# Two weight combinations of the MLP's up projection made by accumulating DMAs, with the signs of the seven-product scheme turned

## The chip, the cores and the metric

The kernel runs on one core of one Trainium2 chip. Its time is the device time of one execution in microseconds; before the change three runs took 1085.81, 1086.14 and 1086.2 us, with a median of 1086.14 us. The profile is of one more execution of the same program. Matrix products run on PE (TensorE), elementwise work on DVE (VectorE) and ACT (ScalarE); POOL (GpSimd) and SP (SyncE) issue DMAs or do small things. Each engine works through its own queue in the order in which the program put its instructions, and engines wait for each other and for DMAs by semaphores.

## The reference

The program is a decoder trunk of two layers over 512 tokens and a width of 1024: one layer with multi-head latent attention, one with gated linear attention, each followed by a squared-ReLU MLP with 4096 hidden units. Only the MLP is touched:

```python
def sq_relu_mlp(xn, w_up, w_down):
    hid = jnp.square(jax.nn.relu(xn @ w_up))
    return hid @ w_down

for i in range(DEPTH):                      # DEPTH = 2
    ...                                     # x = x + mixer(rms_norm(x))
    x = x + sq_relu_mlp(rms_norm(x, norm_mlp[i]), mlp_w_up[i], mlp_w_down[i])
return rms_norm(x, final_norm)
```

`w_up` is 1024x4096 and `w_down` 4096x1024 in each layer, all float32.

## The kernel before

**Precision.** Every float32 operand of a product is split into a rounded high part (`wh`, written by ACT with a Copy, L104) and the rest (`wl`, written by DVE with a subtraction, L107). An ordinary product then takes three matmuls (`mm3`, L109: high by high, high by low, low by high).

**The MLP.** `mlp` (L793) cuts the 4096 hidden units into eight blocks of 512. The first block's up projection is done plainly by `up` (L801). Meanwhile `quadrants` (L890) combines the four quadrants of the normed activations (two halves of the width by two halves of the tokens) into four combinations, in four `comb` tiles `t1` to `t4`, and splits each into a kept tile `T1` to `T4` (L904 to L907). The seven other blocks go through `up_fast` (L909). It does the block's up projection by the two-by-two scheme of Winograd, with seven products instead of eight. The block's weights are four quadrants of 512x256: `a11` and `a12`, the upper and lower half of the first loaded tile `raw[0]`, and `a21` and `a22`, the halves of `raw[1]`. DVE makes four combinations of them:

- `s1 = a21 + a22` (L958) and `s2 = s1 - a11` (L959), each in a `comb` tile;
- `s4 = a12 - s2` (L969) in a third `comb` tile;
- `a11 - a21` (L970), written over `a21`.

`product` (L916) splits one of the seven weight tiles and runs sixteen matmuls, eight with 512 columns (L923) and eight with 256 (L924). The order on PE is `a11`, one tile of the down projection, `a12`, `s2`, two down tiles, `a11 - a21`, `s1`, one down tile, `s4`, `a22`, four down tiles. These down tiles belong to the block before (`down`, L823; `others(n)` steps it n tiles on); each sums into a PSUM bank `b`, of which there are three, and DVE adds it to the residual `xT` (L837), which frees the bank. `total` (L934) and `finish` (L945) join the products, apply the ReLU and the row scale (L947), square, and split.

**Buffers and queues.** Weights come by SP's queue (`load`, L132), 1 MB each, into `wraw` with two buffers, and `raw` for one down chunk of each block. A load waits until DVE has made the last `wl` out of the tile that lay in its buffer. `wh` and `wl` have three buffers each, `comb` has four. In `up`, the two chunks of the plain block take two weight pieces each; the second piece of the second chunk has its `wl` made in the middle of PE's work on that chunk, and the load of the first fast block's `raw[1]` (SP, L134) waits for this `wl`, since it goes into the same buffer.

**Who sets the order.** A scheduler gives each engine its order when the program is built, by its own estimate of when operands are ready; program order only breaks ties. So an instruction can stand on an engine ahead of work that comes earlier in the text.

Of the kernel before, what the change touches and what calls it, by code (L numbers as in the profile page):

```python
# [14 lines left out]
AF = mybir.ActivationFunctionType  # L15
ALU = mybir.AluOpType
AX = mybir.AxisListType

P = 128
# [5 lines left out]
FB = 512  # L25
TH = S // 2
# [24 lines left out]
def trunk_kernel(ctx: ExitStack, tc: tile.TileContext, t_in: dict, out: bass.AP, out_row: bass.AP):  # L51
    nc = tc.nc
    PE, ACT, DVE, POOL, SP = nc.tensor, nc.scalar, nc.vector, nc.gpsimd, nc.sync
# [5 lines left out]
    def uname(s):  # L59
        count[0] += 1  # L60
        return f"{s}_{count[0]}"
# [17 lines left out]
    def two_banks(tag):  # L79
        return psum["pool"].tile([P, 1024], F32, tag=f"ps_{tag}", bufs=1, name=uname("ps2"))  # L80
# [8 lines left out]
    def tmp(shape=(P, 512), dt=F32):  # L89
        return sb.tile(list(shape), dt, tag="tmp", bufs=6, name=uname("tmp"))  # L90

    def slot(tag, shape=(P, 512)):
        return sb.tile(list(shape), F32R, tag=f"set_{tag}", bufs=16, name=uname("set"))
# [5 lines left out]
    def f(ap):  # L99
        return ap.bitcast(F32)  # L100

    def split(src, hi, lo, hi_eng=ACT, lo_eng=DVE, order=lambda i: i):
        if hi_eng is ACT:
            order(ACT.activation(hi, src, AF.Copy))  # L104
        else:
            hi_eng.tensor_copy(hi, src)
        lo_eng.tensor_tensor(lo, src, f(hi), ALU.subtract)  # L107
# [24 lines left out]
    def load(src, a, n):  # L132
        raw = sb.tile([P, a, n], F32, tag="wraw", bufs=2, name=uname("wraw"))
        SP.dma_start(raw, src)  # L134
        return raw

    def piece(raw, a, n, order=lambda i: i):
        hi = sb.tile([P, a, n], F32R, tag="wh", bufs=3, name=uname("wh"))
        lo = sb.tile([P, a, n], F32R, tag="wl", bufs=3, name=uname("wl"))
        split(raw, hi, lo, order=order)  # L140
        return hi, lo

    def cut(pair, *idx):
        return tuple(t[idx] for t in pair)
# [56 lines left out]
    def gcol(name, j):  # L201
        c = GAIN_COL[name] + j
        return gains[:, c : c + 1]
# [84 lines left out]
    nrm = Norm(ND, inv_dr, "mix", 0)  # L288
# [81 lines left out]
    def col_chunk(w2d, c0, n):  # L370
        return load(w2d[:, c0 : c0 + n].rearrange("(k p) n -> p k n", p=P), w2d.shape[0] // P, n)
# [421 lines left out]
    def mlp(layer, nrm, tag, nxt, final=False):  # L793
        w_up, w_dn = t_in["mlp_w_up"][layer], t_in["mlp_w_down"][layer]
# [88 lines left out]
        KH = ND // 2  # L883

        def comb():
            return fast.tile([P, KH, 256], F32, tag="comb", bufs=4, name=uname("comb"))
# [3 lines left out]
        def quadrants():  # L890
            lead, trail = range(KH), range(KH, ND)
            quad["11"] = [nrm.parts[k][:, :, first] for k in lead]
            quad["21"] = [nrm.parts[k][:, :, first] for k in trail]
            quad["22"] = [nrm.parts[k][:, :, second] for k in trail]
            t1, t2, t3, t4 = comb(), comb(), comb(), comb()
            for k in lead:
                g1, g2 = (gcol(nrm.g, nrm.g0 + j) for j in (k, k + KH))
                u, v = xT[k], xT[k + KH]
                ACT.activation(t3[:, k], u[:, second], AF.Copy, scale=g1)
                DVE.scalar_tensor_tensor(t3[:, k], v[:, second], g2, t3[:, k], ALU.mult, ALU.subtract)  # L900
                DVE.scalar_tensor_tensor(t2[:, k], u[:, first], g1, t3[:, k], ALU.mult, ALU.add)
                DVE.scalar_tensor_tensor(t4[:, k], v[:, first], g2, t2[:, k], ALU.mult, ALU.subtract)
                DVE.scalar_tensor_tensor(t1[:, k], v[:, second], g2, t2[:, k], ALU.mult, ALU.subtract)
            for name, t in (("T2", t2), ("T3", t3), ("T1", t1), ("T4", t4)):  # L904
                parts = fast.tile([P, KH, 2, TH], F32R, tag=name, name=uname(name))
                split(t, parts[:, :, 0], parts[:, :, 1])
                quad[name] = [parts[:, k] for k in lead]  # L907

        def up_fast(b, others):  # L909
            raw = [col_chunk(w_up, b * FB + c * 256, 256) for c in range(2)]  # L910
            a11, a12 = raw[0][:, :KH], raw[0][:, KH:]
            a21, a22 = raw[1][:, :KH], raw[1][:, KH:]
            halves = [(slot(tag), slot(tag)) for _ in range(4)]


            def product(t, a, q, start):  # L916
                w = piece(a, KH, 256)
                for j in range(2):
                    o = t[:, j * 512 : (j + 1) * 512]
                    for k in range(KH):  # L920
                        wh, wl = cut(w, slice(None), k, slice(j * P, (j + 1) * P))
                        x = quad[q][k]
                        PE.matmul(o.rearrange("p (h t) -> p h t", h=2), wh, x, start=start and k == 0, stop=False, skip_group_check=True)  # L923
                        PE.matmul(o[:, :TH], wl, x[:, 0], start=False, stop=k == KH - 1, skip_group_check=True)  # L924

            def parts(t):
                v = t.rearrange("p (j h t) -> p h j t", j=2, h=2)
                return v[:, 0], v[:, 1]

            def by_tile(v):  # L930
                return v.rearrange("p (j t) -> p j t", j=2)


            def total(t, term=None):  # L934
                high, low = parts(t)
                r = tmp()
                if term is None:
                    ACT.activation(by_tile(r), low, AF.Copy)
                else:
                    DVE.tensor_tensor(by_tile(r), low, by_tile(term), ALU.add)  # L940
                DVE.tensor_tensor(by_tile(r), high, by_tile(r), ALU.add)  # L941
                return r


            def finish(c, half, tk):  # L945
                c3 = by_tile(c)
                DVE.scalar_tensor_tensor(c3, c3, 0.0, nrm.rstd[:, tk].unsqueeze(1).to_broadcast([P, 2, TH]), ALU.max, ALU.mult)  # L947
                ACT.activation(c, c, AF.Square)
                for j in range(2):
                    hi, lo = halves[2 * half + j]  # L950
                    split(c3[:, j], hi[:, tk], lo[:, tk])

            z, y = two_banks("z"), two_banks("y")
            product(z, a11, "11", True)
            others(1)
            p1 = total(z)
            s1, s2 = comb(), comb()
            DVE.tensor_tensor(s1, a21, a22, ALU.add)  # L958
            DVE.tensor_tensor(s2, s1, a11, ALU.subtract)  # L959
            product(y, a12, "21", True)  # L960
            c11 = total(y, p1)
            product(z, s2, "T2", False)
            others(2)
            u = total(z)
            finish(c11, 0, first)
            s4 = comb()

            with tc.issue_after(quad["hid"]) if b == 1 else nullcontext():
                DVE.tensor_tensor(s4, a12, s2, ALU.subtract)  # L969
                DVE.tensor_tensor(a21, a11, a21, ALU.subtract)  # L970
            product(z, a21, "T3", False)
            v = total(z)
            y = two_banks("y")
            product(y, s1, "T1", True)
            others(1)
            c22 = total(y, v)
            product(y, s4, "22", False)
            product(z, a22, "T4", False)
            finish(c22, 1, second)
            c12 = total(y, u)  # L980
            finish(c12, 0, second)
            c21 = total(z)
            finish(c21, 1, first)
            others(4)
            return halves

        hid = up()
        quadrants()
        for b in range(NB):
            if b + 1 < NB:  # L990
                tiles = down(b, hid)

                def others(n):
                    for _ in range(n):
                        next(tiles)

                hid = up_fast(b + 1, others)
                continue
            es.close()
            if final:  # L1000
                psum_layout(False)
                down_final(b, hid)
            else:
                for _ in down(b, hid):
                    pass
# [571 lines left out]
```

## Time and profile before

| what | before |
|---|---|
| median of three runs | 1086.14 us |
| profiled execution, first to last instruction (span) | 1084.4 us |
| PE busy | 1075.7 us, 99% of the span |
| DVE busy | 859.6 us, 79% |
| ACT busy | 549.2 us, 51% |
| POOL busy | 43.4 us, 4% |
| moved by DMA | 101.61 MB, 94 GB/s on the mean |

What lies around the profiled span, 1086.1 less 1084.4, is 1.7 us. A row of a group gives the busy time and the mean length of one instruction, then the engine's idle time just before them and what ended most of it. A row of the timeline gives start, length, engine, line, operation and tiles, with the idle time before it in brackets. SPq is SP's queue: its rows are the issues of DMAs. PE overlaps one matmul with the next, so that the length of one (0.39 us for 512 columns) is more than the step from one start to the next (some 0.23 us).

### The profile page before, as it was taken

What the parts mean: (1) busy time and instruction counts of PE and PEld (TensorE: products, weight loads), DVE (VectorE), ACT (ScalarE), POOL (GpSimd) and SP (SyncE); (2) the same over time, 40 slices, a digit from 0 to 9 for tenths busy, and PEclk for the clock granted to TensorE, in tenths of its full rate; (3) what the DMA queues carried; (4) which work ended last, traced back from release to release, by engine and by line L of the source; (5) the groups of instructions that cost most, each with busy time, mean ns of one, the idle gap of its engine ahead of it and who ended that gap; (6) DMA issues with size and microseconds to landing.
All of it is one profiled execution on the core that took longest, in us unless ns stands there. A gap on an engine that the chain in (4) does not pass through costs nothing.

```text
span 1084.4 us, 14045 instructions
## 1 busy us (share of the span) xinstructions
PE 1075.7 (99%) x5372; PEld 909.5 (84%) x5372; DVE 859.6 (79%) x1426; ACT 549.2 (51%) x927; POOL 43.4 (4%) x72
## 2 busy tenths in 40 slices
PE   9999999999999999999999999999999999999997
PEld 7888888888888888888788888888888888888886
DVE  7899968987887887977686584569888797797875
ACT  7767654553453453455345736556445345344354
POOL 8310002000000000000000000000000000000000
PEclk9999999999999999999999999999999999999999
DMA  7311232142332332322322222232233233223122
GB/s 225 88 50 39 79 117 78 61 134 78 117 117 78 117 117 78 110 84 79 90 76 78 78 78 75 70 127 67 90 115 119 79 101 123 87 80 125 69 97 78
DMA packets 86195, 101.61 MB, mean 94 GB/s; under 512 B 7440, under 2 KB 64016, under 8 KB 86128
## 3 DMA queue, kind: packets, MB, share of 16 engines
q1 hardware_dynamic: 84320, 99.67, 28.5%
q10 hardware_dynamic: 1808, 1.05, 0.3%
q8 instruction: 42, 0.69, 0.3%
q14 instruction: 25, 0.20, 0.1%
HBM read 98.35 MB, written 2.10 MB: 93 GB/s over the span
## 4 chain that ended last, share of the span: by engine, by line
PE 97%; DVE 1%; DMA 0%; ACT 0%; issue 0%; SPq 0%; DVEq 0%; ACTq 0%
PE ps L112 21%; PE ps L114 21%; PE ps L113 21%; PE ps L923 17%; PE ps L924 9%; PE ps L1201 2%; PE ps L129 1%; PE ps L408 1%; PE ps L871 1%; PE ps L1272 0%; PE ps L671 0%; PE ps L1251 0%; PE ps L667 0%; PE ps L670 0%; DMA gains<-in_gains_dram 0%; PE ps L669 0%
## 5 line engine op out<-in xcount | busy, mean ns | idle before, releaser
L112 PE MATMUL ps<-set,wh 128*128 128x512 f32 x760 | 296.8, 391 | 0.0
L113 PE MATMUL ps<-set,wh 128*128 128x512 f32 x760 | 296.6, 390 | 0.0
L114 PE MATMUL ps<-set,wl 128*128 128x512 f32 x760 | 296.3, 390 | 0.0
L104 ACT ACTIVATE wh<-wraw 128x1024 fp32r<-128x1024 f32 x139 | 147.0, 1061 | 240.8 <-PE ps L113 115.2
L107 DVE TENSOR_TENSOR wl<-wraw,wh 128x1024 fp32r<-128x1024 f32 x139 | 169.9, 1222 | 41.8 <-ACT wh L104 41.5
L114 PEld LDWEIGHTS ps<-set,wl 128*128 128x128 f32 x760 | 142.7, 188 | 30.3 <-DVE wl L107 0.2
L112 PEld LDWEIGHTS ps<-set,wh 128*128 128x128 f32 x760 | 142.7, 188 | 29.8
L113 PEld LDWEIGHTS ps<-set,wh 128*128 128x128 f32 x760 | 142.8, 188 | 27.6
L923 PE MATMUL ps<-T,wh 128*128 128x512 f32 x448 | 157.5, 391 | 0.0
L924 PE MATMUL ps<-T,wl 128*128 128x256 f32 x448 | 126.2, 282 | 0.0
L923 PE MATMUL ps<-set,wh 128*128 128x512 f32 x336 | 119.9, 397 | 0.0
L923 PEld LDWEIGHTS ps<-T,wh 128*128 128x128 f32 x448 | 84.1, 188 | 18.2
L924 PE MATMUL ps<-set,wl 128*128 128x256 f32 x336 | 94.2, 280 | 0.0
L107 DVE TENSOR_TENSOR wl<-comb,wh 128x1024 fp32r<-128x1024 f32 x42 | 51.4, 1223 | 47.7 <-ACT wh L104 47.7
L837 DVE TENSOR_TENSOR xT<-ps,xT 128x512 f32<-128x512 f32 x120 | 82.3, 686 | 7.1 <-PE ps L114 7.1
L104 ACT ACTIVATE wh<-comb 128x1024 fp32r<-128x1024 f32 x42 | 44.6, 1061 | 83.2 <-PE ps L923 81.8
L924 PEld LDWEIGHTS ps<-T,wl 128*128 128x128 f32 x448 | 84.6, 189 | 0.5
L923 PEld LDWEIGHTS ps<-set,wh 128*128 128x128 f32 x336 | 63.1, 188 | 15.1
L941 DVE TENSOR_TENSOR tmp<-ps,tmp 128x512 f32<-128x512 f32 x98 | 67.2, 686 | 0.9
L924 PEld LDWEIGHTS ps<-set,wl 128*128 128x128 f32 x336 | 63.4, 189 | 1.6
L112 PE MATMUL ps<-wh,set 128*128 128x512 f32 x144 | 58.8, 408 | 0.0
L104 ACT ACTIVATE wh<-raw 128x1024 fp32r<-128x1024 f32 x28 | 29.6, 1055 | 56.7 <-PE ps L923 55.7
(362 smaller groups left out, 1662.3 us busy)
## 6 DMA issues: line engine op xcount, KB each, us to landing
wraw<-in_mlp_w_up_dram SPq DMA_DIRECT2D x32, 1024.0 KB, 5.4
wraw<-in_mlp_w_down_dram SPq DMA_DIRECT2D x18, 1024.0 KB, 5.0
raw<-in_mlp_w_down_dram SPq DMA_DIRECT2D x14, 1024.0 KB, 5.1
wraw<-in_gla_w_in_dram SPq DMA_DIRECT2D x12, 1024.0 KB, 5.2
wraw<-in_mla_w_o_dram SPq DMA_DIRECT2D x4, 1024.0 KB, 5.2
wraw<-in_gla_w_o_dram SPq DMA_DIRECT2D x4, 1024.0 KB, 5.2
xT<-in_x_dram SPq DMA_DIRECT2D x6, 256.0 KB, 5.1
wraw<-in_mla_w_in_dram SPq DMA_DIRECT2D x3, 512.0 KB, 7.1
```

The source lines that it names most:

```text
L104: order(ACT.activation(hi, src, AF.Copy))
L107: lo_eng.tensor_tensor(lo, src, f(hi), ALU.subtract)
L112: PE.matmul(psum, wh, xh, start=start, stop=False)
L113: PE.matmul(psum, wh, xl, start=False, stop=False)
L114: PE.matmul(psum, wl, xh, start=False, stop=stop)
L129: PE.transpose(psum, src, ident[: src.shape[0], : src.shape[0]])
L408: PE.matmul(p, w[:, i, j * P : (j + 1) * P], x, start=start, stop=stop)
L837: DVE.tensor_tensor(xT[m], p, xT[m], ALU.add)
L923: PE.matmul(o.rearrange("p (h t) -> p h t", h=2), wh, x, start=start and k == 0, stop=False, skip_group_check=True)
L924: PE.matmul(o[:, :TH], wl, x[:, 0], start=False, stop=k == KH - 1, skip_group_check=True)
L941: DVE.tensor_tensor(by_tile(r), high, by_tile(r), ALU.add)
L1201: PE.matmul(p[:, t - t0], k[:, t * P : (t + 1) * P], moving[:, t], start=True, stop=True)
```

## The change

`s1` is no longer made by DVE. A plain 512 KB load on SP's queue brings `a22` into a `comb` tile, and a DMA on POOL's queue with an accumulating write adds `a21` to it. In the same way `raw[1]` is loaded as before, and a second accumulating DMA from POOL adds `a11` onto its upper half, so that `s3 = a11 + a21` stands there. For these to be sums, signs are turned: `s1` is as it was, `s3` is a sum instead of a difference, `s2 = s1 + a11` and `s4 = a12 + s2`. The activations' combinations T2, T1 and T4 are negated when they are split, and the ReLU of the second half of a block takes the minimum instead of the maximum, since its sums come out negated before they are squared.

The changed lines move the numbers of what lies behind them: what was L947 is L958 after, L837 stays, L959 becomes L969, L969 becomes L979, L923 and L924 become L933 and L934, L940 and L941 become L950 and L951.

```diff
-            for name, t in (("T2", t2), ("T3", t3), ("T1", t1), ("T4", t4)):
+            for name, t, sign in (("T2", t2, -1.0), ("T3", t3, 1.0), ("T1", t1, -1.0), ("T4", t4, -1.0)):
                 parts = fast.tile([P, KH, 2, TH], F32R, tag=name, name=uname(name))
-                split(t, parts[:, :, 0], parts[:, :, 1])
+                hi, lo = parts[:, :, 0], parts[:, :, 1]
+                ACT.activation(hi, t, AF.Copy, scale=sign)
+                DVE.scalar_tensor_tensor(lo, t, sign, f(hi), ALU.mult, ALU.subtract)
                 quad[name] = [parts[:, k] for k in lead]
 
         def up_fast(b, others):
+            def quadrant(c, h):
+                cs = slice(b * FB + c * 256, b * FB + c * 256 + 256)
+                return w_up[h * KH * P : (h + 1) * KH * P, cs].rearrange("(k p) n -> p k n", p=P)
+
             raw = [col_chunk(w_up, b * FB + c * 256, 256) for c in range(2)]
+            s1 = comb()
+            SP.dma_start(s1, quadrant(1, 1))
             a11, a12 = raw[0][:, :KH], raw[0][:, KH:]
-            a21, a22 = raw[1][:, :KH], raw[1][:, KH:]
+            s3, a22 = raw[1][:, :KH], raw[1][:, KH:]
+            POOL.dma_start(s1, quadrant(1, 0), accum_op=ALU.add)
+            POOL.dma_start(s3, quadrant(0, 0), accum_op=ALU.add)
...
-                DVE.scalar_tensor_tensor(c3, c3, 0.0, nrm.rstd[:, tk].unsqueeze(1).to_broadcast([P, 2, TH]), ALU.max, ALU.mult)
+                clip = ALU.min if half else ALU.max
+                DVE.scalar_tensor_tensor(c3, c3, 0.0, nrm.rstd[:, tk].unsqueeze(1).to_broadcast([P, 2, TH]), clip, ALU.mult)
...
-            s1, s2 = comb(), comb()
-            DVE.tensor_tensor(s1, a21, a22, ALU.add)
-            DVE.tensor_tensor(s2, s1, a11, ALU.subtract)
+            s2 = comb()
+            DVE.tensor_tensor(s2, s1, a11, ALU.add)
...
             with tc.issue_after(quad["hid"]) if b == 1 else nullcontext():
-                DVE.tensor_tensor(s4, a12, s2, ALU.subtract)
-                DVE.tensor_tensor(a21, a11, a21, ALU.subtract)
-            product(z, a21, "T3", False)
+                DVE.tensor_tensor(s4, a12, s2, ALU.add)
+            product(z, s3, "T3", False)
```

## The prediction

> **What bounds the kernel now.** I read the page first: busy shares, the chain that ended last, and the groups of the changed stage.
>
> ```profile
> span 1084.4 us, 14045 instructions
> PE 1075.7 (99%) x5372; PEld 909.5 (84%) x5372; DVE 859.6 (79%) x1426; ACT 549.2 (51%) x927; POOL 43.4 (4%) x72
> ...
> PE 97%; DVE 1%; DMA 0%; ACT 0%; issue 0%; SPq 0%; DVEq 0%; ACTq 0%
> ...
> L923 PE MATMUL ps<-T,wh 128*128 128x512 f32 x448 | 157.5, 391 | 0.0
> L924 PE MATMUL ps<-T,wl 128*128 128x256 f32 x448 | 126.2, 282 | 0.0
> L923 PE MATMUL ps<-set,wh 128*128 128x512 f32 x336 | 119.9, 397 | 0.0
> ```
>
> PE carries 97% of the chain, and the products that the change feeds were issued with no idle time before them (the last column). Then I cut four fast blocks out of the first layer (one starts every 41.4 us); the columns are length of the stretch, then busy time and count for PE, weight loads, DVE, ACT and POOL, then clock, DMA share and GB/s.
>
> ```profile
> 205.00:246.30 41.30, 41.30 (x209) 35.09 (x208) 36.44 (x50) 20.68 (x32) 0.00 (x0) 1.00 0.30 102
> 246.30:287.70 41.40, 41.40 (x209) 35.19 (x208) 32.90 (x45) 18.49 (x28) 0.00 (x0) 1.00 0.32 102
> 287.70:329.10 41.40, 41.40 (x209) 35.18 (x208) 35.21 (x47) 18.48 (x27) 0.00 (x0) 1.00 0.31 102
> 329.10:370.50 41.40, 41.40 (x209) 35.19 (x208) 33.92 (x46) 18.50 (x27) 0.00 (x0) 1.00 0.32 102
> ```
>
> PE is busy through every block at full clock. DVE's load differs by 3.5 us between blocks and the block stays within 0.1 us: DVE does not set its length. So taking work off DVE can win nothing in a block; only a new wait can change the time, and it changes it for the worse. The question is which of the new DMAs land too late. PE's own order, as the built program has it, is the same matmuls in the same sequence before and after.
>
> **What leaves DVE.** The two additions, once a block, 14 blocks.
>
> ```profile
> L958 DVE TENSOR_TENSOR comb<-wraw x14: 1212/1226/1228, 202.8 to 1006.0; 128x1024 f32<-128x1024 f32 x14
> ...
> L970 DVE TENSOR_TENSOR wraw<-wraw,wraw x14: 1214/1218/1220, 212.5 to 1011.3; 128x1024 f32<-128x1024 f32 x14
> ```
>
> That is 14 times (1.226 + 1.218), 34.2 us of DVE's 859.6. Covered by PE it is worth 0 us. The sign changes cost nothing by themselves: scale and clip are immediates of instructions that were there. The eight splits of T1 to T4 go from a two-input subtraction to a three-operand form.
>
> ```profile
> 743.71 0.75 DVE L250 SCALAR_TENSOR_TENSOR set<-xT,gains,set 128x512 fp32r<-128x512 f32 x1
> 744.38 0.69 DVE L239 TENSOR_TENSOR acc<-acc,tmp 128x512 f32<-128x512 f32 x1
> ```
>
> The nearest pair of rows is 0.69 us against 0.75 us at 512 columns, so a 1024-column split takes between 0 and some 0.15 us more; four in a row move DVE by at most 0.6 us, where it has 1.5 us to spare (worked out below).
>
> **What the DMAs cost.** New per block: a plain 512 KB load on SP, two accumulating 512 KB DMAs on POOL; over 14 blocks 22 MB beside 101.61, on queues that are 0.3 busy in a block. SP's 14 issues and POOL's 28 stand on queues with room (POOL does nothing in the four blocks). What matters is the time from issue to landing, and the trace has no DMA from POOL and none that accumulates. The nearest rows:
>
> ```profile
> wraw<-in_mla_w_in_dram SPq DMA_DIRECT2D x1, 512.0 KB, 4.5
> rstd<-rstd SPq DMA_DIRECT2D x4, 64.0 KB, 2.0
> wraw<-in_mla_w_in_dram SPq DMA_DIRECT2D x3, 512.0 KB, 7.1
> 21.10 0.80 POOL L336 TENSOR_TENSOR rope<-rope,rope 128x128 f32<-128x128 f32 x1
> wraw<-in_mlp_w_up_dram SPq DMA_DIRECT2D x32, 1024.0 KB, 5.4
> ```
>
> The first row is one 512 KB load with the queue to itself (the stretch at 13 us), the third the median of three with the start's crowd. The plain load of `a22` I take at 4.5 us. For the accumulating one, the lower end is the same 4.5 us; the upper end is two crowded loads in series, 14.2 us. My value, an estimate: a small on-chip move shows 2.0 us that do not depend on size, so a load of 512 KB has 2.5 us of data; an accumulation must also read what lies there, 5.0 us; and POOL's software adds about one of its small instructions, 0.8, rounded to 1. Sum 8.0 us.
>
> [...]
>
> **A block in the middle: covered.** In the built order SP issues the load for the next block's `s1` right behind `raw[1]` of this one, a whole block ahead; POOL then does this block's `s3` and the next one's `s1`.
>
> ```profile
> 354.23 5.43 SPq L134 DMA_DIRECT2D wraw<-in_mlp_w_up_dram  x2
> 359.19 0.68 DVE L941 TENSOR_TENSOR tmp<-ps,tmp 128x512 f32<-128x512 f32 x1
> 364.75 1.23 DVE L958 TENSOR_TENSOR comb<-wraw 128x1024 f32<-128x1024 f32 x1 [0.24 <-DMA wraw<-in_mlp_w_up_dram]
> 370.54 0.39 PE L923 MATMUL ps<-set,wh 128*128 128x512 f32 x1
> 381.80 1.06 ACT L104 ACTIVATE wh<-wraw 128x1024 fp32r<-128x1024 f32 x1 [1.71 <-PE ps L923]
> 387.18 0.40 PE L923 MATMUL ps<-T,wh 128*128 128x512 f32 x1
> ```
>
> `raw[1]` landed at 364.7, where DVE's wait ended. `s3` would land 8 us later, at 372.7, and ACT splits it at 381.80 for the product at 387.18: 9 us to spare on ACT, and about 12 on PE (387.18 less 1.06 of ACT and 1.23 of DVE is 384.9). The next `s1` is queued behind it on POOL and has a further block of 41 us. `s2` now stands earlier on DVE, right behind the L941 of 359.19, and needs `raw[0]`, issued at 354.23 and landed some 5.4 us later, 359.6: just in time. If it were late, the split of `a11` for the product at 370.54 would be next, four instructions on, some 3.6 us; that leaves 7 us. Cost of these blocks: 0 us. Gone is the cover only if an accumulation takes 20 us.
>
> **The first fast block of each layer: not covered.** Here there is no block ahead. The load of `a22` goes into the `comb` buffer of `t3`, so SP waits for DVE's split of T3. On DVE's queue the built order has `s2`, which waits for POOL's DMA, directly behind the third instruction of the norm's root (L215), and ahead of L814 and of the `wl` for the second half of the plain block's second chunk, which PE needs in the midst of running. First layer:
>
> ```profile
> 186.97 1.28 DVE L107 TENSOR_TENSOR T<-comb,T 128x1024 fp32r<-128x1024 f32 x1
> 194.55 0.69 DVE L215 SCALAR_TENSOR_TENSOR rstd<-tmp,tmp 128x512 f32<-128x512 f32 x1
> 195.35 0.69 DVE L814 SCALAR_TENSOR_TENSOR tmp<-ps,rstd 128x512 f32<-128x512 f32 x1
> 195.96 1.22 DVE L107 TENSOR_TENSOR wl<-wraw,wh 128x1024 fp32r<-128x1024 f32 x1
> 199.68 0.19 PEld L114 LDWEIGHTS ps<-set,wl 128*128 128x128 f32 x1
> ...
> 327.31 1.22 DVE L959 TENSOR_TENSOR comb<-comb,wraw 128x1024 f32<-128x1024 f32 x1
> 328.44 1.22 DVE L970 TENSOR_TENSOR wraw<-wraw,wraw 128x1024 f32<-128x1024 f32 x1
> ```
>
> The split of T3 ends at 188.25; the load lands 4.5 later, 192.75; the accumulation at 200.75. That is when `s2` can start. DVE was there at 195.24 and stands still. Behind `s2`: its own step of 1.13 (from the start of L959 to that of L970), L814 with 0.61 (195.35 to 195.96), and the `wl` with 1.22, together 2.96 us. PE loads this `wl` at 199.68, so `s2` must start by 196.72. It starts 4.03 us late, and PE waits 4.0 us. (DVE's spare time above is 196.72 less 195.24.) Second layer:
>
> ```profile
> 745.37 1.22 DVE L107 TENSOR_TENSOR T<-comb,T 128x1024 fp32r<-128x1024 f32 x1
> 752.75 0.69 DVE L215 SCALAR_TENSOR_TENSOR rstd<-tmp,tmp 128x512 f32<-128x512 f32 x1
> 758.25 0.19 PEld L114 LDWEIGHTS ps<-set,wl 128*128 128x128 f32 x1
> ...
> 221.52 0.40 PE L923 MATMUL ps<-T,wh 128*128 128x512 f32 x1
> ```
>
> 746.59 + 4.5 + 8.0 is 759.09, the deadline 758.25 less 2.96, 755.29: 3.8 us. Nothing gives it back, for PE has no idle time behind it. Next in line is late in step with it: `raw[1]` of that block waits for this same `wl`, so it and its `s3` move with PE, and `s3` keeps some 6 us: 5.4 of load and 8.0 of accumulation are 13.4 after that `wl`, and in the first layer the product of `s3` came at 221.52, 21.8 after the weight load at 199.68, of which ACT and DVE take 2.3 for the split.
>
> **Sum.** 4.0 + 3.8 = 7.8 us on the profiled 1084.4: a span of 1092.2, and on the median of 1086.1, 1094 us.
>
> **Rivals.**
>
> *No wait.* If load and accumulation together take no more than 8.5 us (196.72 less 188.25), DVE comes through in time. At the lower ends, 4.5 + 4.5, the waits are 0.5 and 0.3 us: 1086.1 to 1086.9. For it: nothing in the block slows a DMA, and a 1 MB load takes 5.4. Against: two operands are read, and a small POOL instruction alone took 0.8 us. [...] Chance 0.19.
>
> *Every block waits.* From 20 us of accumulation on, `s3` is late at 384.9 in every block. At 22 us it costs 2 us in each of the twelve later blocks and at least 18 in each first one: 60 us, 1146. The upper row is 14.2, so chance 0.05.
>
> *Faster.* The products on `set` tiles take 397 ns against 391 on T tiles; if that were DVE reading beside PE, 336 times 6 ns, 2.0 us, or a little more, could come back, and if the waits were also covered it would be 1084 or less. It decides only where the difference follows DVE's load, and the four blocks, 3.5 us of DVE apart, say no. Chance 0.04.
>
> That the additions stay on DVE can be left out: the built order has 28 instructions fewer there.
>
> **Numbers.** The forecast, a wait in the first fast block of each layer only, has the remaining 0.72. Its own range: accumulation from 5.1 to 14.2 us, 1088 to 1107 (twice 14.2 less 4.1 is 20.2). The whole range reaches down to the case of no wait, 1085.8 (the lowest run), and up to 1107. A measurement of this kernel tells 0.2%, 2.2 us, from no change; 5.1 us of accumulation is where two waits reach that. So slower 0.77 (forecast and every block), same 0.19, faster 0.04.
>
> **What would show it.** In the profile after: accumulating DMAs at some 8 us to landing; DVE waiting at `s2` twice, some 5.5 us each, for a DMA into `comb`; PE waiting twice, some 4 us each, at L114 for DVE's `wl`, near 200 and near 762 us; fast blocks still 41.4 us long; DVE some 34 us less busy. It is wrong if PE waits in later blocks, if the accumulation lands within 5 us, or if a block's length moves with DVE's load.

## The result, and the profile after

| | before | after |
|---|---|---|
| median of five runs | 1086.14 us (1085.81 to 1086.52) | 1089.4 us (1089.17 to 1091.29) |
| profiled execution: time, span | 1086.1, 1084.4 us | 1091.29, 1089.6 us |
| DVE busy | 859.6 us | 828.1 us |
| moved by DMA | 101.61 MB | 123.63 MB |

The changed kernel is slower: ratio 1.0032, 95% interval 1.0021 to 1.0042, which is 3.3 us. The forecast was 7.9 us more than before: the sign and the place were right, the size was less than half of it. A second set of five runs, beside the last experiments, gave 1091.06 us against 1086.34, 1.0046 (1.0034 to 1.0059). So the loss is 3 to 5 us. The profiled execution is the slowest of the first five; the other four had spans up to 1088.1.

From the page of after: the busy line, the chain's shares by engine, the one group of PE with a wait, the software DMA queue, and the new DMAs with their size and median time to landing.

```profile
PE 1076.7 (99%) x5372; PEld 909.3 (83%) x5372; DVE 828.1 (76%) x1398; ACT 550.2 (50%) x927; POOL 77.7 (7%) x100
q0 software_dynamic: 14784, 14.68, 8.8%
PE 93%; DMA 2%; DVE 2%; POOL 1%; issue 1%; ACT 0%; SPq 0%; POOLq 0%; DVEq 0%
L114 PE MATMUL ps<-set,wl 128*128 128x512 f32 x760 | 296.5, 390 | 4.1 <-DVE wl L107 4.1
L933 PE MATMUL ps<-set,wh 128*128 128x512 f32 x336 | 119.9, 397 | 0.0
comb<-in_mlp_w_up_dram POOLq DMA_DIRECT2D x14, 512.0 KB, 7.2
wraw<-in_mlp_w_up_dram POOLq DMA_DIRECT2D x14, 512.0 KB, 5.8
```

PE's share of the chain fell from 97% to 93%; DMA, DVE and POOL now hold 5 points of it, where DVE alone held 1: some stretches now end on transfers. L114 had no idle time in the page before and has 4.1 us now, behind a `wl` of DVE. The view of waits says how often:

```profile
DVE comb L969 <- DMA comb<-in_mlp_w_up_dram: 8.0, 2, 4.2
PE ps L114 <- DVE wl L107: 4.1, 2, 2.4
```

Two waits of DVE at `s2` (total, times, longest), each followed by one of PE at L114: one for each layer. The blocks themselves did not move. The first and the last window of four blocks of the first layer, with the columns of the prediction's fence:

```profile
208.20:249.60 41.40, 41.40 (x210) 35.17 (x209) 34.55 (x47) 20.84 (x32) 5.14 (x4) 1.00 0.62 160
...
332.40:373.80 41.40, 41.40 (x209) 35.19 (x208) 31.73 (x43) 18.60 (x27) 2.56 (x2) 1.00 0.51 140
```

DVE has about 2 us less to do in a block, DMAs are busy 0.5 to 0.6 instead of 0.3 of the time, and PE still fills 41.40 of 41.40 us.

Now the first of the two waits, link by link, from the chain of waits of after (start, length, what).

```profile
188.88 3.73 DMA comb<-in_mlp_w_up_dram
...
192.65 0.58 issue
...
193.25 6.78 DMA comb<-in_mlp_w_up_dram
...
200.05 0.03 DVE comb L969
200.09 1.11 issue
201.19 0.68 DVE tmp L814
201.88 1.15 DVE wl L107
```

The plain load of `a22` goes out at 188.88, as DVE's split of T3 frees the buffer (the first row of the next fence, 187.53 and 1.28: 188.81), and lands 3.73 us later; POOL's DMA starts 0.64 us after that and lands 6.78 us later; `s2`, L814 and the `wl` follow on DVE, and PE goes on at 203.06. The rows of that place in the timeline give the idle time, and the same rows of the second layer follow.

```profile
187.53 1.28 DVE L908 SCALAR_TENSOR_TENSOR T<-comb,T 128x1024 fp32r<-128x1024 f32 x1
...
200.05 1.23 DVE L969 TENSOR_TENSOR comb<-comb,wraw 128x1024 f32<-128x1024 f32 x1 [4.25 <-DMA comb<-in_mlp_w_up_dram]
203.06 0.50 PE L114 MATMUL ps<-set,wl 128*128 128x512 f32 x1 [2.44 <-DVE wl L107]
...
749.89 0.37 SPq L918 DMA_DIRECT2D comb<-in_mlp_w_up_dram  x1
754.18 1.28 POOL L921 DMA_DIRECT2D comb<-in_mlp_w_up_dram  x1 [285.13 <-DMA comb<-in_mlp_w_up_dram]
760.51 1.23 DVE L969 TENSOR_TENSOR comb<-comb,wraw 128x1024 f32<-128x1024 f32 x1 [3.79 <-DMA comb<-in_mlp_w_up_dram]
763.52 0.50 PE L114 MATMUL ps<-set,wl 128*128 128x512 f32 x1 [1.61 <-DVE wl L107]
```

2.44 and 1.61 us, 4.05 in all, where the prediction had 4.03 and 3.8. (PE's idle time counts from the modelled end of the matmul before, which is 0.39 long, while its step to the next is 0.23: each wait costs some 0.16 us more than its idle time, both together 4.4. The span of this execution grew by 5.2. Of the rest, 0.56 us lies at the kernel's start, which the change does not touch: there the chain of after begins with a load of `xT` that lands at 8.00, the chain of before with one of `gains` that lands at 4.77.)

### The profile page after: what moved, and what is told of

It reads as the page before. It is cut to its first block, busy times and chain, and to the rows that moved or that the text cites. A ratio compares the mean times of both kernels' runs of the same rounds, so it can differ in the third digit from the quotient of the medians.

```text
span 1089.6 us, 14147 instructions
## 1 busy us (share of the span) xinstructions
PE 1076.7 (99%) x5372; PEld 909.3 (83%) x5372; DVE 828.1 (76%) x1398; ACT 550.2 (50%) x927; POOL 77.7 (7%) x100
## 2 busy tenths in 40 slices
DMA packets 108372, 123.63 MB, mean 113 GB/s; under 512 B 8113, under 2 KB 86193, under 8 KB 108305
## 3 DMA queue, kind: packets, MB, share of 16 engines
q0 software_dynamic: 14784, 14.68, 8.8%
## 4 chain that ended last, share of the span: by engine, by line
PE 93%; DMA 2%; DVE 2%; POOL 1%; issue 1%; ACT 0%; SPq 0%; POOLq 0%; DVEq 0%
PE ps L114 20%; PE ps L112 20%; PE ps L113 20%; PE ps L933 17%; PE ps L934 9%; DMA comb<-in_mlp_w_up_dram 2%; PE ps L1210 2%; PE ps L129 1%; PE ps L871 1%; PE ps L408 1%; DVE wl L107 1%; DMA xT<-in_x_dram 0%; PE ps L1281 0%; PE ps L671 0%; PE ps L1260 0%
## 5 line engine op out<-in xcount | busy, mean ns | idle before, releaser
L114 PE MATMUL ps<-set,wl 128*128 128x512 f32 x760 | 296.5, 390 | 4.1 <-DVE wl L107 4.1
L107 DVE TENSOR_TENSOR wl<-wraw,wh 128x1024 fp32r<-128x1024 f32 x139 | 169.8, 1221 | 38.7 <-ACT wh L104 38.3
L114 PEld LDWEIGHTS ps<-set,wl 128*128 128x128 f32 x760 | 142.7, 188 | 35.0 <-DVE wl L107 4.9
L933 PE MATMUL ps<-T,wh 128*128 128x512 f32 x448 | 157.5, 391 | 0.0
L934 PE MATMUL ps<-T,wl 128*128 128x256 f32 x448 | 126.2, 282 | 0.0
L933 PE MATMUL ps<-set,wh 128*128 128x512 f32 x336 | 119.9, 397 | 0.0
L837 DVE TENSOR_TENSOR xT<-ps,xT 128x512 f32<-128x512 f32 x120 | 82.3, 686 | 23.3 <-PE ps L114 23.3
L107 DVE TENSOR_TENSOR wl<-comb,wh 128x1024 fp32r<-128x1024 f32 x42 | 51.4, 1223 | 63.4 <-ACT wh L104 63.4
L933 PEld LDWEIGHTS ps<-T,wh 128*128 128x128 f32 x448 | 84.1, 188 | 18.2
L934 PE MATMUL ps<-set,wl 128*128 128x256 f32 x336 | 94.2, 280 | 0.0
L934 PEld LDWEIGHTS ps<-T,wl 128*128 128x128 f32 x448 | 84.6, 189 | 0.5
L933 PEld LDWEIGHTS ps<-set,wh 128*128 128x128 f32 x336 | 63.1, 188 | 15.1
L951 DVE TENSOR_TENSOR tmp<-ps,tmp 128x512 f32<-128x512 f32 x98 | 67.2, 686 | 1.0
L934 PEld LDWEIGHTS ps<-set,wl 128*128 128x128 f32 x336 | 63.4, 189 | 1.6
```

The costliest lines, as they stand in the source:

```text
L114: PE.matmul(psum, wl, xh, start=False, stop=stop)
L837: DVE.tensor_tensor(xT[m], p, xT[m], ALU.add)
```

## The experiments

Each starts from the changed kernel. "Before" ran beside each set: 1086.32 us with the first four, 1086.34 us with the others.

### s2 behind the `wl`

```diff
-            DVE.tensor_tensor(s2, s1, a11, ALU.add)
+            with tc.issue_after(quad["wl"]) if b == 1 else nullcontext():
+                DVE.tensor_tensor(s2, s1, a11, ALU.add)
```

`quad["wl"]` is the last `wl` that `up` makes for the plain block's second chunk. Nothing else changes: the same DMAs, at the same place.

> Only DVE's order in the first fast block of each layer changes: s2 stands behind the wl of the plain block's second chunk. Theory (the whole loss is PE's wait for that wl, queued behind s2): PE waits at L114 go from 4.1 us to 0 and the time is that of before, 1086.1 +/- 0.4 us. Rival (the added DMA traffic or POOL's work costs a little in every block): some 1089 us as in the changed kernel, with fast blocks longer than 41.4 us.

1086.39 us, ratio 0.9999 (0.999 to 1.0008). The loss is gone. The timeline of this kernel (lines here are 3 or 4 higher, so `s2` is L973):

```profile
192.90 1.46 POOL L924 DMA_DIRECT2D comb<-in_mlp_w_up_dram  x1 [4.29 <-DMA comb<-in_mlp_w_up_dram]
...
196.19 1.22 DVE L107 TENSOR_TENSOR wl<-wraw,wh 128x1024 fp32r<-128x1024 f32 x1
...
200.26 1.22 DVE L973 TENSOR_TENSOR comb<-comb,wraw 128x1024 f32<-128x1024 f32 x1
```

The accumulation starts as in after, the `wl` is out at 196.19 instead of 201.79, and `s2` comes at 200.26 with no wait in front of it. So the DMA's length costs nothing by itself; what cost was the place of the waiting instruction ahead of the `wl` on DVE's queue.

### The first block's sums on DVE, the others by DMA; and the reverse

```diff
-            s1 = comb()
-            SP.dma_start(s1, quadrant(1, 1))
-            POOL.dma_start(s1, quadrant(1, 0), accum_op=ALU.add)
-            POOL.dma_start(s3, quadrant(0, 0), accum_op=ALU.add)
+            by_dma = b > 1
+            s1 = comb()
+            if by_dma:
+                SP.dma_start(s1, quadrant(1, 1))
+                POOL.dma_start(s1, quadrant(1, 0), accum_op=ALU.add)
+                POOL.dma_start(s3, quadrant(0, 0), accum_op=ALU.add)
...
+            if not by_dma:
+                DVE.tensor_tensor(s1, s3, a22, ALU.add)
...
+                if not by_dma:
+                    DVE.tensor_tensor(s3, a11, s3, ALU.add)
```

> In the first fast block of each layer s1 and s3 are sums on DVE as before; the twelve later blocks use the accumulating DMAs. Theory: 1086.1 +/- 0.4 us, no PE wait at L114. Rival (a cost spread over the 14 blocks): 12/14 of the 3.3 us stay, 1089 us.

1086.5 us, ratio 1.0001 (0.9992 to 1.001). Twelve of fourteen blocks with their DMAs cost nothing, and nothing is won by the 24 additions that left DVE. The reverse has `by_dma = b == 1`:

> The reverse: accumulating DMAs in the first fast block of each layer alone, sums on DVE in the twelve others. Theory: the whole loss stays, 1089.4 +/- 0.7 us, with two PE waits of some 2.5 and 1.7 us. Rival (spread cost): 2/14 of 3.3 us, 1086.6 us.

1090.7 us, ratio 1.0041 (1.0028 to 1.0053). All of the loss comes back with four accumulating DMAs out of 28, and its two waits of PE are those of after, a little shorter:

```profile
PE ps L114 <- DVE wl L107: 3.4, 2, 1.7
```

1090.7 lies above the band expected from after's first 1089.4. That could mean that the later DMAs win back a microsecond, so the changed kernel ran again beside the next set:

> The changed kernel once more, beside the next three, so that all share the same runs of the kernel before; in the run without the later DMAs the loss was 4.4 us, in the changed kernel's first run 3.3 us. Theory (the two waits in the first fast blocks are all of the loss): 1089.4 to 1090.7, so 3.2 to 4.5 us above the kernel before, and two waits of PE at L114 of 3.4 to 4.1 us in sum. Rival (the later DMAs win back about a microsecond by relieving DVE): again 1089.4 or less, clearly below 1090.7, and with the same waits as that run.

1091.06 us, a shade over what either theory gave, with 4.0 us of PE waits at L114 in two. It is not below 1090.7, so nothing is won back; the difference between the two sets of runs is how well a loss of 3 to 5 us repeats.

### POOL's DMAs copy instead of adding

```diff
-            POOL.dma_start(s1, quadrant(1, 0), accum_op=ALU.add)
-            POOL.dma_start(s3, quadrant(0, 0), accum_op=ALU.add)
+            POOL.dma_start(s1, quadrant(1, 0))
+            POOL.dma_start(s3, quadrant(0, 0))
```

> POOL's 28 DMAs copy instead of adding (the weight combinations s1 and s3 are then only their second operand). Theory of the size (2.0 us fixed, 2.5 of data, as much again for the second read, the rest POOL's own): the first one lands some 2.0 to 2.5 us earlier than the 6.8 us of the adding one, at some 4.5 us, PE's waits shrink to about 0.4 and 0 us, time 1086.1 to 1086.8. Rival (the price is POOL's issue, reading twice is nothing): 6.3 to 6.8 us to landing, 1089 us.

1087.12 us, ratio 1.0007 (0.9998 to 1.0016), 0.3 us over the range expected. The kernel leaves out both additions of every block, so its weight combinations are not the right ones. Its page, with the rows that stand for the adding ones above, and its chain and timeline in the first layer:

```profile
q0 software_dynamic: 4032, 14.68, 4.5%
comb<-in_mlp_w_up_dram POOLq DMA_DIRECT2D x14, 512.0 KB, 5.2
wraw<-in_mlp_w_up_dram POOLq DMA_DIRECT2D x14, 512.0 KB, 4.2
```

```profile
188.72 3.85 DMA comb<-in_mlp_w_up_dram
...
193.20 4.54 DMA comb<-in_mlp_w_up_dram
```

```profile
200.78 0.50 PE L114 MATMUL ps<-set,wl 128*128 128x512 f32 x1 [0.32 <-DVE wl L107]
```

This measures two terms of the prediction by themselves. A DMA from POOL that only copies takes 4.54 us, 0.69 more than SP's load of the same size right ahead of it in this trace (3.85), and it starts some 0.6 us after that load has landed: POOL's part is 1.3 us. Adding takes 2.24 us more (6.78), in the medians 2.0 and 1.6. And the wait follows the landing: 2.24 us less of DMA, 2.12 us less of wait. (The span of this execution is 1.0 us above before's; the wait is half of it, and the other half lies at the kernel's start, as in after.) For the same 14.68 MB the queue handles 14784 packets instead of 4032 and is busy 8.8% instead of 4.5%. The busy share doubles; the time to landing rises by half only, from 4.54 to 6.78. Doubling all of the 4.54 but the 2.0 us of the small on-chip move in the prediction (`rstd`) would give 7.1, an estimate.

### A fifth `comb` buffer

```diff
-            return fast.tile([P, KH, 256], F32, tag="comb", bufs=4, name=uname("comb"))
+            return fast.tile([P, KH, 256], F32, tag="comb", bufs=5, name=uname("comb"))
```

> Five comb buffers in place of four: the load of s1 in the first fast block has its own buffer and does not wait for the split of T3. Theory (the chain from that split through load and accumulation is what is late): the load starts with the other loads of the block before 185 us, s1 is complete before DVE reaches s2, no wait of PE at L114, 1086.0 to 1086.8. Rival (the accumulating DMA disturbs DVE or the weight path wherever it lies): the loss of 3 us stays, 1089 to 1090.

1086.53 us, ratio 1.0002 (0.9993 to 1.0011). The timeline:

```profile
169.67 0.57 SPq L918 DMA_DIRECT2D comb<-in_mlp_w_up_dram  x1
176.72 1.45 POOL L921 DMA_DIRECT2D comb<-in_mlp_w_up_dram  x1 [97.68 <-DVE comb L901]
193.96 1.22 DVE L969 TENSOR_TENSOR comb<-comb,wraw 128x1024 f32<-128x1024 f32 x1
```

With its own buffer the load goes out 19 us earlier, the sum is there some 11 us before DVE comes to `s2` (the accumulation landed after 6.2 us), and `s2` does not wait although it stands even earlier in DVE's order. So the wait needs both: the buffer shared with T3 and the place on DVE. All 28 accumulating DMAs run in this kernel, and all 28 additions are off DVE; it ties with the kernel before.

### s3 accumulated two, three and four times in the later blocks

```diff
-            POOL.dma_start(s3, quadrant(0, 0), accum_op=ALU.add)
+            for _ in range(1 if b == 1 else 2):
+                POOL.dma_start(s3, quadrant(0, 0), accum_op=ALU.add)
```

This asks how much cover the later blocks have. In the other two kernels the 2 is a 3 and a 4.

> In the twelve later blocks the DMA that adds a11 onto s3 is done twice in series (so s3 is a21 plus twice a11: the up projection's weights are other ones there). Theory (from the prediction: in a later block s3 has 9 us to spare behind an accumulation of 8, so up to about 17 us are covered on ACT and 20 on PE): two take some 6 + 0.6 + 6 = 12 to 13 us, which is still covered, blocks of 41.4 us, 1089 to 1091 like the changed kernel. Rival (POOL's DMAs take room from SP's loads or are near the limit): PE waits at the products on set tiles in the later blocks, 1 us or more in each, 1101 or more.

> The same with four in series in each later block (s3 is a21 plus four times a11). Theory: some 4 times 5.8 to 6.6 = 23 to 26 us from the landing of raw[1], 3 to 6 us past the 20 us that PE's product leaves, so PE waits 3 to 6 us in each of the twelve later blocks and the time is 1125 to 1160, with blocks of 44 to 47 us. Rival (the cover is larger than the prediction worked out, since ACT and DVE split ahead or the order shifts): below 1100; rival (smaller): 1170 or more.

Two: 1090.41 us, ratio 1.0042 (1.0028 to 1.0055), the loss of after and no more. PE's waits are the two of the first blocks, although the DMAs slow each other: the next `s1`'s, issued 0.75 us behind the second of a pair (250.36 and 249.61), has a median of 11.2 us, against 7.2 in after. From the page, the waits and the DMA view of the kernel with two:

```profile
span 1088.2 us, 14161 instructions
PE 1076.5 (99%) x5372; PEld 909.6 (84%) x5372; DVE 827.7 (76%) x1398; ACT 550.0 (51%) x927; POOL 95.1 (9%) x112
PE ps L114 <- DVE wl L107: 3.3, 2, 1.8
comb<-in_mlp_w_up_dram POOLq DMA_DIRECT2D x14, 512.0 KB, 11.2
```

Four: 1249.99 us, ratio 1.1532 (1.1501 to 1.1563), 90 us over the top of the range. The same views, with the wait that is new, at the products of the later blocks (it names L952, `total`'s addition, which empties the bank `z` that these products write):

```profile
span 1243.0 us, 14186 instructions
PE 1103.3 (89%) x5372; PEld 928.1 (75%) x5372; DVE 826.3 (66%) x1398; ACT 548.5 (44%) x927; POOL 125.9 (10%) x136
PE ps L934 <- DVE tmp L952: 128.0, 12, 12.8
```

Two things were more than expected. The first is the DMAs, as the chain of waits of this kernel shows:

```profile
242.90 1.28 POOL wraw L923
...
249.25 9.16 DMA wraw<-in_mlp_w_up_dram
...
258.69 9.23 DMA wraw<-in_mlp_w_up_dram
...
268.20 5.87 DMA wraw<-in_mlp_w_up_dram
```

The second and the third take over 9 us, the fourth 5.87; POOL's queue lets the next block's `s1` go between, whose median is 11.2 us in this run too. From the first start to the last landing it is 31.2 us, not 26. Behind the landing at 274.07 come ACT's split, DVE's `wl` and then L952 before PE goes on at 277.20: 3.1 us, where the prediction counted 2.3 for the split alone. The second is the clock. Windows of this kernel, with the wait, the 4 us behind it, and what follows:

```profile
264.80:277.20 12.40, 0.00 (x0) 0.00 (x0) 1.88 (x3) 2.94 (x5) 1.28 (x1) 0.60 0.49 76
277.20:279.00 1.80, 1.80 (x5) 1.59 (x6) 1.80 (x3) 0.80 (x2) 0.00 (x0) 0.50 0.00 0
279.00:281.30 2.30, 2.30 (x9) 1.93 (x8) 1.15 (x3) 0.00 (x0) 0.00 (x0) 0.55 0.00 0
281.30:283.00 1.70, 1.70 (x12) 1.50 (x11) 0.00 (x0) 1.07 (x2) 0.00 (x0) 1.00 0.00 0
```

After 12.4 us without a product, PE's granted clock (the third column from the right) is 0.50 for 1.8 us and 0.55 on the mean of the next 2.3, then 1.00: 5 matmuls in 1.8 us, and later 12 in 1.7. Does a wait half as long cost clock too? For that came the run with three:

> Three accumulations of a11 onto s3 in series in each later block (s3 is a21 plus three times a11). From the runs with two and four: s3 has to be complete some 19 us after raw[1] lands, the second of two in series is complete at 16.0, the third of four stood at 25.3. Theory: PE waits 6 us in each of the twelve later blocks, 75 us, and if a wait of 6 us costs granted clock as the waits of 11 to 12 us did (PE's busy time grew by 27 us in the run with four), up to 25 more: 1163 to 1190. Rival (no clock is lost after waits this short, as after the 2.4 us of the changed kernel): 1155 to 1168, with PE's busy time at 1077.

```profile
PE 1101.2 (94%) x5372; PEld 926.2 (79%) x5372; DVE 826.1 (70%) x1398; ACT 548.4 (47%) x927; POOL 110.5 (9%) x124
PE ps L934 <- DVE tmp L952: 61.4, 12, 6.3
273.19 0.80 PE L934 MATMUL ps<-T,wh 128*128 128x512 f32 x1 [5.91 <-DVE tmp L952]
273.20:277.00 3.80, 3.80 (x12) 3.22 (x13) 2.93 (x5) 0.78 (x2) 0.00 (x0) 0.50 0.00 0
277.00:281.00 4.00, 4.00 (x21) 3.53 (x20) 1.43 (x2) 1.55 (x2) 0.00 (x0) 0.84 0.00 0
```

Its two executions took 1153.67 and 1176.86 us, too far apart for a time of its own; the profile is of the longer one. Its twelve waits at L934 sum to 61.4 us, the longest 6.3. Behind the one of 5.91 us the clock is at half for 3.8 us and more; over the whole execution PE's busy time is 24.5 us above after's 1076.7, and the mean clock is 0.968. The shorter execution lost clock too: its mean is 0.979, against 0.998 to 0.999 in those of the changed kernel's first five. After the 2.44 us of the changed kernel the clock stays full (a row from its windows, with the wait's end at 203.06):

```profile
203.00:206.00 3.00, 2.94 (x13) 2.44 (x14) 2.96 (x6) 2.42 (x4) 0.00 (x0) 1.00 0.56 159
```

But the length of the wait alone does not decide. The same run with three has a wait of 1.82 us at L114 in the first fast block, and a clock of 0.51 on the mean of the 3.4 us from 203.15:

```profile
202.35 0.50 PE L114 MATMUL ps<-set,wl 128*128 128x512 f32 x1 [1.82 <-DVE wl L107]
203.15:206.55 3.40, 3.40 (x10) 2.63 (x9) 3.31 (x4) 2.05 (x3) 0.00 (x0) 0.51 0.90 277
```

So a wait of 1.82 us had slower matmuls behind it in one execution, and one of 2.44 us in another had not. What decides it is open.

Half clock through the 3.4 us of that window costs 1.7 us, and lowers the mean clock of an execution of 1089 us by 0.0016. The four executions with a mean of 0.997 (1091.69 and 1092.69 of the changed kernel's second set, 1091.32 of the reverse, 1092.43 of the run with two) are the slowest of their sets. So the two waits may now and then cost clock in the changed kernel as well, which would be part of its spread; no trace of these four is kept, and it is not shown.

No kernel of the study is faster than the one before. In the two that remove the wait and keep all the DMAs (`s2` moved, the fifth buffer), PE is busy 99% of the span, as before, and DVE's 31 us are not on the way.

## Why the prediction was off in size

**That PE bounds the kernel and DVE's relief is worth nothing: right.** The tie of the kernels with `s2` moved and with the fifth buffer is this step measured. DVE is 31.5 us less busy, not 34.2; 28 times the step of 1.13 us that the prediction read between two starts is 31.6, so the step, not the length, was the thing to multiply. The rival that was faster falls with it: the products on `set` tiles take 397 ns after as before. The three-operand splits take 1224 ns on the mean, as the subtractions did before (L908 and L107, eight of each), ACT's part of them 1050 ns in both traces, and the ReLU with the turned clip 684 ns against 687.

**That later blocks are covered: right.** Two accumulations in series are still covered. In the run with three, the last one landed at 270.1 (issued at 261.28, 8.8 us) and PE waited 5.91 us, so it was due at 264.2; `raw[1]` had landed at 244.8. The cover is 19.4 us, against "takes 20 us"; the difference is L952, which the prediction left out. The price given for that rival, 60 us, left the clock out: in the run with four, waits of 128.0 us and 26.8 us of slower products (1103.3 less 1076.5 of PE's busy time) are the whole 154.8 us between the spans of four and two.

**That the first fast block of each layer is not covered: right, with the chain named:** T3's split, SP's load, POOL's accumulation, `s2`, L814, `wl`, L114. Three edits break it at three links (the place of `s2`, the buffer, the DMA itself), and each comes within 0.1% of the kernel before.

**The sum is where it failed.** In the first layer, from T3's split to the landing (predicted times are those of the trace before; after began 0.56 us later):

| term | predicted | measured |
|---|---|---|
| load of `a22` | 4.5 | 0.07 to its issue and 3.73 |
| accumulation, with POOL's start | 8.0 | 0.64 and 6.78 |
| `s2` to the product | 2.96 | 3.03 with the gap at landing |
| time available, from T3's split | 11.43 | 11.81 |
| wait of PE | 4.03 | 2.44 |

The second layer is the same with 3.73, 0.56 and 6.30: its wait is 1.61 where 3.8 was forecast. The load term failed by 0.7 us: the 4.5 was one load at the kernel's start, and this one was quicker. The accumulation term failed by 0.6 and 1.1 us. Its parts in the first layer, by the copying run: the plain pass, taken at 4.5, is 3.85; the addition, priced at 2.5 as a second read, is 2.24; POOL's part, priced at 1.0, is 1.33. That 2.0 us of a load do not depend on its size, that the addition's time is a second read and that POOL's is software were the prediction's estimates; the runs show the three lengths, not what they consist of. The deadline was taken at the weight load, which in the trace before stands 0.22 us ahead of its product (199.68 and 199.90), and idle time counts from an end that is 0.16 later still: together the 0.38 of the fourth row. Each error is small against its term, but the wait is what is left of 15.5 us above 11.4: errors of 1.6 and 2.2 us took half of it. The prediction's own range for the accumulation, 5.1 to 14.2 us for this case, held the 6.3 to 6.8.

The table explains 4.4 of the 7.8 us forecast, for the profiled execution, which lost 5.2 us; the median one lost 3.3. What the wait is there can be judged from kernels whose first fast blocks are the same: in the reverse and in the runs with two and four, the two waits sum to 3.4, 3.3 and 3.1 us; in the changed kernel's second trace they sum to 4.0. The shortest accumulation onto `s1` takes 6.3 us in after, 6.2 in the run with two and 6.0 in the run with three. So both differ from one execution to the next, the sum of the waits by 1.0 us. Why it does is open.

**The rival without a wait** needed load and accumulation within 8.5 us; they took 11.2 and 10.6. Of its lower ends of 4.5 and 4.5, the load, at 3.73, was quicker; the accumulation, at 6.3 to 6.8 behind a start of 0.6, was not, and 4.54 is what the copying run's DMA took without the addition.

## What to carry to other kernels

In this kernel, with PE busy 99% of the span, moving 31 us of DVE's work to DMAs won nothing (1086.39 and 1086.53 us where nothing waited, against 1086.3), and it lost 3.3 to 4.7 us where the first instruction that waits for the new transfer stood ahead of work that PE needs soon: look for that instruction on each engine's queue, in the first turn of every loop above all, where nothing was issued ahead. One more buffer, or a place behind the `wl` in DVE's queue, removed the whole loss here. A wait worked out as a sum of terms less a deadline inherits all of their errors: give its range from the terms, and check the deadline at the instruction that really waits.

## What was not expected of the hardware

- An accumulating DMA from POOL starts 0.56 to 0.64 us after SP's load that it waits for has landed (0.28 us after another DMA of POOL, in the run with four). With a second one issued 0.75 us behind it, one took 9.1 us (in the run with two), and the `s1` DMAs that are issued second have a median of 11.2 us, against 7.2 in after.
- PE's granted clock was 0.50 behind a wait of 12.4 us (the run with four) and behind one of 5.91 us (the run with three), and PE's busy time grew by 26.8 and 24.5 us in these two runs, each with twelve waits at L934. Of two shorter waits, 1.82 us had a clock of 0.51 behind it and 2.44 us one of 1.00. So a wait of some 2 us had a second price once, and its length alone does not tell when.
